# Sum jobs kept out of the stretch from attention's end to the end of the values' block, and the second half of that block's input forms queued behind attention's output product

## The chip, the core and the metric

The kernel runs on one core of one Trainium2 chip, in one launch. The metric is the device time of that launch in microseconds. Engines: PE (TensorE, matmuls), PEld (its weight loads), DVE (VectorE), ACT (ScalarE), POOL (GpSimd) and SP (SyncE, which here only issues transfers). Each engine works through its own list of instructions in order. A DMA is issued from the list of SP, ACT or POOL, and is carried out by the core's 16 DMA engines.

## The reference

Two layers of a decoder trunk on 512 tokens of width 1024, in float32, and a final normalization. The heart of a layer:

```python
h = rmsnorm(x, g_mix)
z = h @ w_in
aq, ak, av, rq, rk, rv, rg, ga, gb = jnp.split(z, SPLIT_POINTS, axis=-1)
ya = sliding_window_sink_attention(rope(aq), rope(ak), av, sinks) @ w_a
r = chunkwise_retention(rotate(rq), rotate(rk) * (RET_QK_DIM ** -0.5), rv)
yb = (group_rms(r) * jax.nn.silu(rg)) @ w_b
x = x + (jax.nn.sigmoid(ga) * ya + jax.nn.sigmoid(gb) * yb) @ w_out
x = x + jnp.square(jax.nn.relu(rmsnorm(x, g_mlp) @ w_up)) @ w_down
```

(Names shortened where the shape is plain.) `rv`, the retention's values, is a product of the 512 x 1024 input and a 1024 x 1024 part of `w_in`.

## The kernel before

**Three matmuls for one.** Each float32 product is made of three in a rounded format: a weight and an input are each split into a high and a low part, and `products` (L387 to L389) multiplies high by high, low by high and high by low. A weight comes as units of 128 x 1024 in the fixed order of `unit_order`. SP loads a unit into one of five `raw` tiles; ScalarE copies it into `hi` (L335) and VectorE subtracts into `lo` (L336), `SPLIT` = 3 units ahead of use; loads run `AHEAD` = 4 units ahead of the split.

**Seven products for eight.** The values, and the two large products of the MLP, are computed by blocks in a scheme of Strassen's kind: sums of weight blocks are multiplied by sums of input blocks. The sums of weights are made by DMA alone and lie in memory as `sums_rv`, `sums_up`, `sums_down` and `sums_last`. `sum_steps` is the list of these jobs for one layer, in the order of use: two for the values, then for each of the MLP's eight blocks two of `w_up` and one of `w_down`. A job is two DMAs from POOL's queue: a copy of the first half of the data (L223) and an accumulation of the second half onto it (L226). The accumulation can be issued only when the copy has landed. One step of the list issues the copy of a job and then the accumulation of the job before it.

**What paces them.** `pace` (L242) is called where a result leaves PSUM. On every second call, while the list lasts, it has POOL copy one column of that result into `mark` (L247), so that POOL waits for it, and puts the next step behind this mark on POOL. Before the change it is called, per layer, at the eight chunks of gate a, the eight of the retention's queries and keys, the eight of its gate, the eight of attention's output product (L1132), the eight of gate b, the eight of `mixed` and the eight of the new `x`: 56 calls, 28 steps. The list of layer 0 needs 26 steps, that of layer 1 needs 24.

**The stretch in question.** Attention is a generator of 16 iterations (four blocks of 128 queries, four pairs of heads) and some more that empty its pipeline; its parts are laid between the matmuls of the chunks by `advance`. The code then runs in this order (names as used below): the eight gate chunks; rk0 and rq0 (the retention's head 0); rg0 to rg3 (four chunks of its gate); the rest of attention (`drain`); `turned.load(0)`; rk1 and rq1; `turned.build(0)`; `turned.load(2)`; rg4 and rg5; `turned.build(2)`; attention's output product; the values (`values`); rk2, rq2, rk3, rq3; and so on.

`Turned` makes the sums of input blocks for the values. `load(ks)` fetches two 128 x 1024 tiles `xg` of the layer's input from memory, from POOL's queue (L871). `build(ks)` scales them on ScalarE (L881, four instructions), takes four sums on VectorE (L884 to L887), and makes three splits, each a copy on ScalarE (L407) and a subtraction on VectorE (L408). Both `build` calls stand in a `tc.issue_after` on attention's last split, so their instructions on ScalarE and VectorE come behind it in those engines' lists. `xg` takes two of six large temporary tiles, which the gate's chunks, the tables and attention's results use as well.

Attention's output product is four units of `w_a` with two chunks of 12 matmuls each; VectorE multiplies each chunk into `mixed` (L1131), which gives its PSUM bank back. PE has five such banks. In `values`, `multiply(a, ...)` reads plain input blocks, `multiply(c, turned[1])` is the first to read the sums, from both `build` calls; `add_values` adds two weight blocks (L315) for two of its seven parts.

**Order.** A planner lays out each engine's list from the program's order and dependencies and an estimate of durations; `tc.issue_after(ins)` makes what is inside it come behind `ins` on `ins`'s engine. So the order on an engine can differ from the text, and it is to be read from the trace.

**The last edit's place.** In layer 1, `turn_x` (L1236) writes the layer's `x`, turned, to memory as the start of the output `y`: eight tiles, each copied from PSUM by ScalarE into one of seven temporaries of 128 x 512 (L1248) and sent from POOL (L1249). `gain_tile` is a tile of four such parts, of which the final gain uses the first two.

Of the kernel before, what the change touches and what calls it, by code (L numbers as in the profile page):

```python
# [12 lines left out]
AF = mybir.ActivationFunctionType  # L13
ALU = mybir.AluOpType
# [8 lines left out]
NB = T // P  # L23
# [92 lines left out]
def decoder(ctx, tc, xT, x_first, w_in, w_rv, w_a, w_b, w_out, w_up, w_pair, w_down, w_end, tables, decay, band, g_last, out):  # L116
    nc = tc.nc
# [13 lines left out]
    def temp(name="t"):  # L131
        return tmp.tile([P, T], F32, tag="t", name=name, bufs=7)
# [31 lines left out]
    state = {"next": 0, "loaded": 0, "split": 0, "hold": None}  # L164
# [74 lines left out]
    DONE, steps = object(), []  # L239
    pace_count = [0]  # L240

    def pace(src):  # L242

        pace_count[0] += 1
        if steps and pace_count[0] % 2 == 0:
            mark = small.tile([P, 1], F32, tag="mark", name="mark", bufs=2)
            ins = nc.gpsimd.tensor_copy(mark, src[:, 0:1])  # L247
            with tc.issue_after(ins.ins):
                if next(steps[0], DONE) is DONE:
                    steps.pop(0)  # L250
# [66 lines left out]
    def split_until(n):  # L317
        while state["split"] < min(n, len(order)):
            i = state["split"]
            name, part = order[i][1], order[i][-1]  # L320
            if name == "rv":
                add_values(i)
            load_until(i + AHEAD)
            if name == "pair":
                add_part(i)
            elif name == "block":
                add_block(i)
            raw = raws[i]
            hi = wpool.tile([P, UNIT], F32R, tag="hi", name="hi", bufs=SPLIT + 1)
            lo = wpool.tile([P, UNIT], F32R, tag="lo", name="lo", bufs=SPLIT + 1)  # L330
            for at in (LEFT,) if name == "pair" and part == 3 else halves(i):
                if i == 0 and at.start == 0:
                    nc.vector.tensor_copy(hi[:, at], raw[:, at])
                else:
                    nc.scalar.activation(hi[:, at], raw[:, at], AF.Copy)  # L335
                nc.vector.tensor_tensor(lo[:, at], raw[:, at], f32(hi[:, at]), ALU.subtract)  # L336
            kept = {
                "pair": part < 2,
                "block": name == "block" and part < 4 and order[i][2] < N_BLOCK - 1,
                "rv": name == "rv" and order[i][2] < 4,  # L340
            }
            if not kept.get(name):
                raws.pop(i)
            parts[i] = (hi, lo)
            state["split"] += 1
# [265 lines left out]
    def layer_body(layer):  # L611
# [112 lines left out]
        def attention():  # L724
# [36 lines left out]
            for n in range(NB):  # L761
                w = P if n == 0 else 2 * P
                keys = slice(0, P) if n == 0 else slice((n - 1) * P, (n + 1) * P)
                at = slice(n * P, (n + 1) * P)
                for c in range(4):
                    col = layer * N_Q + 2 * c
                    ps = bank(ps_aux, "score")
# [5 lines left out]
                    sm = temp("sm")  # L773
# [22 lines left out]
                    for g in range(N_KV):  # L796
                        nc.vector.tensor_scalar(s3[:, g, :], s3[:, g, :], rc[:, g : g + 1], None, ALU.mult)
                    pend.append((n, c, sm))
                    if ready and c == 1 + DELAY:
                        weighted(ready.pop())  # L800
                    if len(pend) > DEEP:
# [13 lines left out]
        last_exp, last_split = [], []  # L815
# [11 lines left out]
        mixed = [x[:, c, :] for c in range(KD)]  # L827
# [26 lines left out]
        def qk(h, rate=1.0):  # L854
            chunk("w_in", layer, xs, put_ret(rk, h), rate)
            chunk("w_in", layer, xs, put_ret(rq, h), rate)
# [250 lines left out]
        source = xT if layer == 0 else spill  # L1107
        turned = Turned()
        turned.load(0)
        qk(1)  # L1110
        with tc.issue_after(last_split[0]), tc.issue_after(last_split[1]):
            turned.build(0)
        turned.load(2)
        for i in (4, 5):
            chunk("w_in", layer, xs, put_rg(i))
        with tc.issue_after(last_split[0]), tc.issue_after(last_split[1]):
            turned.build(2)


        aT = [(a_h[:, c, :], a_l[:, c, :]) for c in range(4)]  # L1120
        for u in range(4):
            hi, lo = unit("w_a", layer)
            for j in range(2):
                c = 2 * u + j
                ps = bank(ps_mm, "mm")
                pairs = []
                for k in range(4):
                    cols = slice(k * 256 + j * P, k * 256 + (j + 1) * P)
                    pairs.append(((hi[:, cols], lo[:, cols]), aT[k]))
                products(ps, pairs, True, True)  # L1130
                nc.vector.tensor_tensor(mixed[c], mixed[c], ps, ALU.mult)  # L1131
                pace(mixed[c])  # L1132
        for t in a_t:
            slots.give(*t[1])

        load_decay(0)
        values(turned)
        background.append(retention(0))
        qk(2, 2.0)
        qk(3, 2.0)  # L1140
# [95 lines left out]
        def turn_x(ps, b, i):  # L1236
            for k in range(4):
                nc.tensor.matmul(
                    ps[:, k * P : (k + 1) * P],
                    x[:, 4 * i + k, b * P : (b + 1) * P],  # L1240
                    ident,
                    start=k == 0,
                    stop=k == 3,
                    is_transpose=True,
                    skip_group_check=True,
                )
            t = temp("y")
            nc.scalar.activation(t, ps, AF.Copy)  # L1248
            nc.gpsimd.dma_start(y[:, b, i * T : (i + 1) * T], t)  # L1249

# [541 lines left out]
```

## Time and profile before

| what | us |
|---|---|
| runs before (3): median, lowest, highest | 1491.83, 1490.25, 1492.48 |
| the profiled execution: its time | 1491.67 |
| the profiled execution: its span, first to last instruction | 1489.9 |
| chain of waits: share of PE | 86% |

The span is what the profile shows; the execution's time has 1.8 us around it. Timeline rows read: start, duration, engine, line of the kernel, operation, output and inputs, count, and in brackets the time that the engine stood idle before and what ended it. Rows of the DMA list end with size and microseconds from issue to landing. The page's rows of digits are 40 slices of the span in tenths.

### The profile page before, as it was taken

The numbers are of one execution on the slowest core, as the hardware profiler recorded it, in microseconds if no ns is written. First come the engines' busy times: TensorE is split into PE (matmuls) and PEld (weight loads), VectorE is DVE, ScalarE is ACT, GpSimd is POOL, SyncE is SP. The second block draws the span as 40 slices with busy tenths as digits, with TensorE's granted clock in tenths as the row PEclk, the third lists the DMA queues.
The fourth block names the chain that finished last, engine by engine and source line by source line (L and its number), as shares of the span: only waits on it lengthen the run. The fifth ranks groups of instructions, "written<-read, shape, count | busy, mean of one in ns | idle before, by whom it ended". The sixth has DMA issues, their size and how long they took to land.

```text
span 1489.9 us, 21378 instructions
## 1 busy us (share of the span) xinstructions
PE 1461.6 (98%) x7751; PEld 1259.5 (85%) x7751; DVE 1121.9 (75%) x1697; ACT 942.6 (63%) x1549; POOL 215.5 (14%) x302
## 2 busy tenths in 40 slices
PE   9999999999999999999999998899999999999998
PEld 7888778888889999998888886788888889999997
DVE  6877776866677888888878686768766768888885
ACT  7657555543467777777755574455435677777775
POOL 0101210102101111112101012002020021111120
PEclk9999999999999999999999999999999999999999
DMA  7673993658946777766948559936595277776664
GB/s 258 195 208 109 272 285 111 186 154 251 280 98 195 193 189 193 197 175 197 291 150 239 159 129 243 284 107 178 160 268 185 92 206 193 189 198 183 176 189 146
DMA packets 95867, 287.32 MB, mean 193 GB/s; under 512 B 11152, under 2 KB 11280, under 8 KB 90896
## 3 DMA queue, kind: packets, MB, share of 16 engines
q0 software_dynamic: 33648, 113.26, 34.0%
q1 hardware_dynamic: 61392, 171.37, 33.8%
q8 instruction: 61, 1.00, 0.3%
q10 hardware_dynamic: 720, 1.31, 0.2%
q14 instruction: 46, 0.38, 0.1%
HBM read 246.05 MB, written 107.48 MB: 237 GB/s over the span
## 4 chain that ended last, share of the span: by engine, by line
PE 86%; DMA 7%; ACT 3%; DVE 2%; issue 1%; POOL 0%; SPq 0%; ACTq 0%; DVEq 0%; POOLq 0%
PE mm L387 23%; PE mm L389 23%; PE mm L388 23%; PE b L387 3%; PE b L388 3%; PE b L389 3%; DMA raw<-w_rv_in 2%; DMA xg<-spill 1%; PE mm L402 1%; DMA xg<-xT_in 1%; PE score L770 1%; DVE lo L336 1%; DMA sums_down<-w_down_in 1%; ACT hi L335 1%; PE r L388 1%
## 5 line engine op out<-in xcount | busy, mean ns | idle before, releaser
L335 ACT ACTIVATE hi<-raw 128x1024 fp32r<-128x1024 f32 (+1 forms) x375 | 381.7, 1020 | 302.3 <-PE mm L388 165.5
L336 DVE TENSOR_TENSOR lo<-raw,hi 128x1024 fp32r<-128x1024 f32 (+1 forms) x376 | 437.7, 1172 | 151.9 <-ACT hi L335 150.9
L387 PE MATMUL mm<-xh,hi 128*128 128x512 f32 (+1 forms) x976 | 345.6, 356 | 7.3 <-ACT hi L335 5.4
L388 PE MATMUL mm<-xl,hi 128*128 128x512 f32 (+1 forms) x976 | 345.0, 356 | 0.0
L389 PE MATMUL mm<-xh,lo 128*128 128x512 f32 (+1 forms) x976 | 343.1, 356 | 1.5 <-DVE lo L336 1.5
L387 PE MATMUL mm<-r,hi 128*128 128x256 f32 (+1 forms) x736 | 237.1, 326 | 8.7 <-DVE x L1131 8.2
L389 PE MATMUL mm<-r,lo 128*128 128x256 f32 (+1 forms) x736 | 239.4, 325 | 0.3 <-DVE lo L336 0.3
L388 PE MATMUL mm<-r,hi 128*128 128x256 f32 (+1 forms) x736 | 239.6, 326 | 0.0
L387 PEld LDWEIGHTS mm<-xh,hi 128*128 128x128 f32 x976 | 185.5, 190 | 33.0 <-ACT hi L335 5.7
L389 PEld LDWEIGHTS mm<-xh,lo 128*128 128x128 f32 x976 | 184.7, 190 | 26.8 <-DVE lo L336 2.7
L388 PEld LDWEIGHTS mm<-xl,hi 128*128 128x128 f32 x976 | 185.7, 190 | 24.8
L387 PEld LDWEIGHTS mm<-r,hi 128*128 128x128 f32 x736 | 140.1, 190 | 23.0 <-DVE x L1131 9.0
L388 PEld LDWEIGHTS mm<-r,hi 128*128 128x128 f32 x736 | 140.2, 190 | 13.2
L389 PEld LDWEIGHTS mm<-r,lo 128*128 128x128 f32 x736 | 140.2, 190 | 11.9 <-DVE lo L336 0.5
L1474 POOL DMA_DIRECT2D y<-eu x56 | 62.3, 1351 | 371.5 <-DVE eu L1459 371.5
L388 PE MATMUL mm<-lo,r 128*128 128x512 f32 (+1 forms) x276 | 104.3, 387 | 0.0
L389 PE MATMUL mm<-hi,r 128*128 128x512 f32 (+1 forms) x276 | 101.2, 387 | 0.0
L387 PE MATMUL mm<-hi,r 128*128 128x512 f32 (+1 forms) x276 | 98.7, 391 | 1.8 <-ACT eu L1469 1.3
L387 PE MATMUL b<-hi,r 128*128 128x512 f32 x180 | 70.4, 391 | 0.0
L388 PE MATMUL b<-lo,r 128*128 128x512 f32 x180 | 70.2, 390 | 0.0
L271 DVE TENSOR_TENSOR raw<-raw 128x512 f32<-128x512 f32 x56 | 38.5, 687 | 39.5 <-DMA raw<-w_pair_in 27.2
L389 PE MATMUL b<-hi,r 128*128 128x512 f32 x180 | 67.8, 389 | 0.0
(294 smaller groups left out, 2404.1 us busy)
## 6 DMA issues: line engine op xcount, KB each, us to landing
raw<-w_in_in SPq DMA_DIRECT2D x73, 512.0 KB, 4.8
sums_down<-w_down_in POOLq DMA_DIRECT2D x30, 1024.0 KB, 12.5
sums_up<-w_pair_in POOLq DMA_DIRECT2D x56, 512.0 KB, 10.7
raw<-w_down_in SPq DMA_DIRECT2D x45, 512.0 KB, 7.2
raw<-w_pair_in SPq DMA_DIRECT2D x84, 256.0 KB, 3.6
y<-y POOLq DMA_DIRECT2D x64, 256.0 KB, 9.0
y<-eu POOLq DMA_DIRECT2D x62, 256.0 KB, 8.1
raw<-sums_down SPq DMA_DIRECT2D x30, 512.0 KB, 7.1
```

The lines of the kernel that those rows point to most:

```text
L271: nc.vector.tensor_tensor(raws[i][:, at], last[:, LEFT], last[:, RIGHT], ALU.add)
L335: nc.scalar.activation(hi[:, at], raw[:, at], AF.Copy)
L336: nc.vector.tensor_tensor(lo[:, at], raw[:, at], f32(hi[:, at]), ALU.subtract)
L387: nc.tensor.matmul(ps, ah, bh, start=start and i == 0, stop=False, **more)
L388: nc.tensor.matmul(ps, ah, bl, start=False, stop=False, **more)
L389: latest[0] = nc.tensor.matmul(ps, al, bh, start=False, stop=stop and i == n - 1, **more).ins
L402: latest[0] = nc.tensor.matmul(ps, w[:, cols(j, c)], moving[k][low], start=first, stop=bool(final)).ins
L770: nc.tensor.matmul(ps[:, g * w : (g + 1) * w], q_s[g][:, c, at], part[:, keys], start=i == 0, stop=i == 1)
L1474: nc.gpsimd.dma_start(y[:, 2 * j + m, i * T : (i + 1) * T], t, **how)
```

## The change

```diff
+    quiet = [False]
+
     def pace(src):
 
+        if quiet[0]:
+            return
         pace_count[0] += 1
...
-                    nc.scalar.activation(hi[:, at], raw[:, at], AF.Copy)
+                    state["high"] = nc.scalar.activation(hi[:, at], raw[:, at], AF.Copy).ins
...
                     pend.append((n, c, sm))
+                    if n > 1:
+                        pace(sm)
...
         turned.load(0)
+        quiet[0] = True
         qk(1)
         with tc.issue_after(last_split[0]), tc.issue_after(last_split[1]):
             turned.build(0)
         turned.load(2)
         for i in (4, 5):
             chunk("w_in", layer, xs, put_rg(i))
-        with tc.issue_after(last_split[0]), tc.issue_after(last_split[1]):
-            turned.build(2)
...
-                nc.vector.tensor_tensor(mixed[c], mixed[c], ps, ALU.mult)
-                pace(mixed[c])
+                last_mixed = nc.vector.tensor_tensor(mixed[c], mixed[c], ps, ALU.mult)
+            if u == 1:
+                with tc.issue_after(last_mixed.ins), tc.issue_after(state["high"]):
+                    turned.build(2)
         for t in a_t:
             slots.give(*t[1])
 
         load_decay(0)
         values(turned)
+        quiet[0] = False
...
-            t = temp("y")
+            t = gain_tile[:, 2 + i, :] if b == NB - 1 else temp("y")
```

Four things change. From the first input load of `Turned` to the end of `values`, `pace` does nothing, so no step of the sum jobs is issued from the results in between. In attention's iterations of its third and fourth block (`n > 1`), `pace` is called with the score tile `sm`. The second `build` is traced inside the output product, after its second unit, and its instructions come behind that unit's last multiplication into `mixed` on VectorE and behind the newest whole-unit copy into `hi` on ScalarE. And the last two tiles of `turn_x` go through the free half of `gain_tile`.

## The prediction

> **What bounds the kernel now.** I read the page first, then the waits of the matrix engine, its timeline wherever it stood idle, the windows around those places, and last the timelines of the queues that feed them.
>
> ```profile
> span 1489.9 us, 21378 instructions
> ...
> PE 1461.6 (98%) x7751; PEld 1259.5 (85%) x7751; DVE 1121.9 (75%) x1697; ACT 942.6 (63%) x1549; POOL 215.5 (14%) x302
> ...
> DMA  7673993658946777766948559936595277776664
> ...
> PE 86%; DMA 7%; ACT 3%; DVE 2%; issue 1%; POOL 0%; SPq 0%; ACTq 0%; DVEq 0%; POOLq 0%
> ```
>
> PE is the bound: 1461.6 of 1489.9 us, so nothing that leaves the matmuls alone can win more than the 28.3 us of idle time, plus what the clock loses around it. A slice of the DMA row is 1489.9/40 = 37.2 us. Slices 4 and 5 (149 to 223 us) and 24 and 25 (894 to 969 us) stand at 9, with 3 (112 to 149 us) and 5 just ahead of them. Those pairs are the stretch that the change touches, once in each layer. PE's idle time lies just there:
>
> ```profile
> 170.44 0.50 PE L387 MATMUL mm<-r,hi 128*128 128x512 f32 x1 [2.49 <-DVE x L1131]
> 220.58 0.50 PE L387 MATMUL mm<-xh,hi 128*128 128x512 f32 x1 [2.24 <-ACT hi L335]
> 222.19 0.50 PE L389 MATMUL mm<-xh,lo 128*128 128x512 f32 x1 [0.88 <-DVE lo L336]
> 909.17 0.79 PE L387 MATMUL mm<-r,hi 128*128 128x512 f32 x1 [5.73 <-DVE x L1131]
> 961.20 0.79 PE L387 MATMUL mm<-xh,hi 128*128 128x512 f32 x1 [3.17 <-ACT hi L335]
> 963.07 0.80 PE L389 MATMUL mm<-xh,lo 128*128 128x512 f32 x1 [0.64 <-DVE lo L336]
> 1192.99 0.50 PE L387 MATMUL mm<-hi,r 128*128 128x512 f32 x1 [1.32 <-ACT eu L1469]
> ```
>
> Two kinds of stall, each in both layers. In attention's output product PE waits for VectorE's multiplication into `mixed` (L1131), which frees a bank: 2.49 + 5.73 = 8.22 us. Towards the end of the values' block it waits for the split of a weight: 2.24 + 0.88 + 3.17 + 0.64 = 6.93 us. The clock adds to them:
>
> ```profile
> 222.00:226.00 4.00, 3.81 (x11) 3.04 (x12) 4.00 (x8) 1.47 (x3) 0.00 (x0) 0.65 0.55 189
> 226.00:230.00 4.00, 4.00 (x18) 3.27 (x17) 0.99 (x3) 0.00 (x0) 0.00 (x0) 0.93 0.44 131
> ...
> 910.00:914.00 4.00, 4.00 (x13) 3.13 (x13) 3.53 (x5) 2.34 (x3) 0.56 (x1) 0.67 1.02 251
> ...
> 962.00:966.00 4.00, 3.36 (x8) 2.38 (x8) 4.00 (x7) 1.98 (x4) 0.00 (x0) 0.50 0.67 242
> 966.00:970.00 4.00, 4.00 (x16) 3.22 (x16) 1.87 (x4) 0.00 (x0) 0.00 (x0) 0.84 0.44 141
> ```
>
> (Columns: the stretch, its width, busy time of PE, PEld, DVE, ACT and POOL, granted clock, DMA share, GB/s.) After each of these stalls but the one at 170 the granted clock is low for some microseconds. Width times (1 - clock): 1.40 + 0.28 and 2.00 + 0.64, so 4.3 us behind the values' stalls, and 1.3 us behind the one at 909. The Trainium skill (TensorE: Matmul & The Clock Gate, Part 1: The HAM clock gate) says that the gate halves the clock after an idle window of about 3.4 us; the trace agrees for 5.73 us idle (0.67) and for 2.49 us (no drop), and by that rule a stall that only gets shorter would cost its own length and nothing more.
>
> What is behind the stalls is transfers:
>
> ```profile
> 144.58 14.05 DMA xg<-xT_in
> ...
> 203.40 13.97 DMA raw<-w_rv_in
> ...
> 945.01 10.79 DMA raw<-w_rv_in
> ```
>
> ```profile
> raw<-w_in_in SPq DMA_DIRECT2D x73, 512.0 KB, 4.8
> sums_down<-w_down_in POOLq DMA_DIRECT2D x30, 1024.0 KB, 12.5
> sums_up<-w_pair_in POOLq DMA_DIRECT2D x56, 512.0 KB, 10.7
> ```
>
> On the chain of waits a 512 KB load of the values' weights takes 13.97 and 10.79 us, where the same size takes 4.8 us in the median of `w_in`. Beside them run the sum jobs, on POOL's queue (rows of layer 0):
>
> ```profile
> 137.81 0.64 POOL L247 COPY mark<-late 128x1 f32<-128x1 f32 x1 [44.82 <-ACT late L407]
> 138.38 0.53 POOL L223 DMA_DIRECT2D sums_up<-w_pair_in  x1
> ...
> 139.87 1.09 POOL L223 DMA_DIRECT2D sums_down<-w_down_in  x1
> 144.03 0.85 POOL L226 DMA_DIRECT2D sums_up<-w_pair_in  x1 [3.08 <-DMA sums_up<-w_pair_in]
> 144.58 1.42 POOL L871 DMA_DIRECT2D xg<-xT_in  x2
> ...
> 152.83 0.86 POOL L226 DMA_DIRECT2D sums_down<-w_down_in  x1 [6.20 <-DMA sums_down<-w_down_in]
> 153.60 0.65 POOL L871 DMA_DIRECT2D xg<-xT_in  x1
> ...
> 171.28 0.57 POOL L871 DMA_DIRECT2D xg<-xT_in  x1 [4.63 <-DVE r L408]
> ...
> 202.65 0.81 POOL L226 DMA_DIRECT2D sums_down<-w_down_in  x1 [11.62 <-DMA sums_down<-w_down_in]
> ```
>
> POOL issues in order, so a second half of a job (L226) that waits for its first half holds all behind it. The last row is a 1 MB accumulation that starts 0.75 us ahead of the weight load at 203.40.
>
> **The change part by part.**
>
> *Silence (`quiet`).* Per layer 12 calls of `pace` fall silent: rk1, rq1, rg4, rg5 and the eight chunks of the output product. Every second call makes a step, so 6 steps go: 6 marks, 6 copies, 6 accumulations, between the second group of input loads and the end of the values. One accumulation stays open over the silence. This takes the sum traffic off the values' loads. Need, from the trace: layer 0's load at 203.40 must land early enough to lift 2.24 us, layer 1's at 945.01 3.17 us early; at 4.8 us instead of 13.97 and 10.79 they land 9.2 and 6.0 us early. So I take all of the values' stalls and their clock away: 6.93 + 4.3 = **11.2 us**. Bounds: 0, if the loads are slow for other reasons (SP's own loads alone), and 11.2. I take the upper one because a slice at 9 holds six steps of 1 to 2 MB beside SP's loads.
>
> *Earlier jobs.* Eight calls more per layer, in attention's blocks 2 and 3: 4 steps. POOL stood idle 44.82 us ahead of 137.81 and the DMA row is at 3 there, so the marks and copies cost nothing on PE as long as POOL is free; if it is not, a mark holds its score tile, one of seven temporaries. By the order of the calls four of a layer's steps (3 and 4 or 6, and 7 and 8) are marked by a score tile. A step that follows another closely waits for its copy, 10.7 to 12.5 us by the rows above; a tile behind it is held for what is left of that. I take 0, because a tile waits several iterations for its transpose anyway, and up to 3 us a layer if it binds. In all 26 steps are left of 28; layer 0's list needs 26, layer 1's 24, so all sums are still made, two steps later, long before the blocks that read the last ones.
>
> *`build(2)` queued later.* It is 4 scalings and 3 splits on ScalarE, 4 + 3 operations on VectorE, now behind the product's fourth multiplication on VectorE and behind the newest weight split on ScalarE; no instruction is added. Before, its scalings stood ahead of `build(0)`'s own splits:
>
> ```profile
> 908.59 1.33 ACT L881 ACTIVATE xg<-xg,x 128x512 f32<-128x512 f32 x2 [2.94 <-DMA xg<-spill]
> ```
>
> ```profile
> 902.48 0.69 DVE L884 TENSOR_TENSOR xg<-xg 128x512 f32<-128x512 f32 x1 [8.46 <-ACT xg L881]
> ...
> 908.44 0.68 DVE L1131 TENSOR_TENSOR x<-x,mm 128x512 f32<-128x512 f32 x1
> ...
> 925.93 1.82 DVE L408 TENSOR_TENSOR r<-xg,r 128x512 fp32r<-128x512 f32 x2
> ```
>
> The 2.94 us wait on ScalarE goes. But the first multiplication (908.44), which ends PE's 5.73 us, came out of VectorE's backlog after 8.46 us of waiting for `build(0)`'s input, not for `build(2)`'s. So the product's stalls hang on when the first input loads land. Bounds: 0 (same landing) and 8.22 + 1.3 = 9.5 us (landing 6 us earlier). Nothing in the trace settles POOL's new order, so I take the middle, **4.8 us**. The second input loads need a buffer that `build(0)` frees (171.28 waits for it); the wait moved from ScalarE's queue to behind the product has PE's work of half a product (48 matmuls) and the values' first multiplication (24) over it, which at the spacing of these two rows is 72 x 0.23 = 16.6 us:
>
> ```profile
> 929.99 0.39 PE L387 MATMUL rv<-hi,r 128*128 128x512 f32 x1
> 930.22 0.39 PE L388 MATMUL rv<-lo,r 128*128 128x512 f32 x1
> ```
>
> The first of them is the first matmul of the values' second multiplication, which reads the forms. If that cover is gone, PE waits there (C below).
>
> *`gain_tile` for the last two turned tiles (layer 1).* Two temporaries fewer in the ring. The 1.32 us at 1192.99 is the only stall there; bounds 0 and 1.3, I take **0.4**, as ScalarE had just come from those two copies in its own order and the edit does not move them.
>
> Sum: 11.2 + 4.8 + 0.4 = 16.4 us. Against the profiled execution's own 1491.67 us: 1475.3. That execution lies 0.16 us under the median of the runs (1491.83), so 1475.4 on their scale.
>
> **The rivals.**
>
> *A: POOL's queue holds the first input loads back (slower).* With four steps more before it, the step at rq0 (137.81) starts the third block of `w_down`, 1 MB, and the step at rg1 must accumulate it. Before, that place held a 512 KB job, whose accumulation waited until 144.03 and let the input loads out at 144.58. A 1 MB half takes 12.5 us in the median: 138.4 + 12.5 + 0.8 = 151.7, 7.1 us later, in both layers. If the input loads then take their 14.05 us again, the product's stalls become 9.6 and 12.8 us, with some 1.7 us of clock in layer 0 (as after the stalls at 222): + 15.9, less the 11.2 and 0.4 = + 4.3 us, 1496. It decides from a delay of (11.6 - 1.7) / 2 = 5 us a layer. For it: POOL's rows in that order. Against it: before, the accumulation of a 1 MB job (152.83) was queued behind the first input loads, so the planner that lays out POOL's order may do so again; and later loads would meet a quieter DMA. The Trainium skill (DMA: Bandwidth & Descriptors, Anatomy of one DMA) states that a wait on a semaphore happens on the issuing sequencer before dispatch, not in the DMA engines; the row at 152.83 agrees, and by that rule everything behind such an accumulation is late by its wait.
>
> *B: only the values' stalls go.* The first input loads land as late as before, later issue and quieter DMA cancelling: 11.2 + 0.4, or 8 with a remainder of the moved waits: 1480 to 1484.
>
> *C: the wait moves into the values.* In layer 1 `build(2)`'s first split stood at 925.93 on VectorE, 4.1 us before the second multiplication began (929.99). If PE arrives 7 us earlier and the forms come no earlier, PE waits about 3 us plus 1.3 of clock: of 16.4 us some 12 remain, 1480, inside B's range. Against it: `build(0)` no longer waits 2.94 us, so the buffer, the load and the forms come earlier too.
>
> *D: it does nothing that counts.* SP's own loads saturate the stretch: 1489 to 1493.
>
> **How the numbers follow.** Forecast 0.52 (values' stalls gone, the product's shortened: gains of 11.6 to 21, so 1470.5 to 1480); B and C together 0.25; A 0.15, spread from 1487 to 1499; D 0.08. What a measurement can tell from no change is about 0.2%, 3 us. Faster: 0.52 + 0.25, with a little of A: 0.78. Same: most of D and a part of A: 0.09. Slower: the rest of A: 0.13. The range from 1469 to 1492 leaves out the worse two thirds of A and the edges of the others, less than 2 in 10.
>
> **What would show it.** DMA rows: slices 4, 5, 24, 25 fall below 9, slice 3 rises, POOL shows no `sums_` rows from about 155 to 235 us. Values: no PE wait for L335 or L336 near 220 and 960, the weight load on the chain under 8 us, clock 1.00 there. Product: PE's waits for L1131 together under 8.22 us; A shows as an input load issued near 151 and 891 us behind a waiting `sums_down` accumulation, and L1131 waits above 9 us. C shows as PE waiting for L408 on `r<-xg` before `rv`. The prediction is wrong at its root if the values' loads still take over 10 us without sum jobs beside them, or if the total falls by less than 8 us.

## The result, and the profile after

| what | before | after |
|---|---|---|
| median of 7 runs each, us | 1491.83 (1489.31 to 1494.99) | 1485.09 (1482.37 to 1487.99) |
| ratio, 95% interval | | 0.9956 [0.9939, 0.9972] |
| the profiled execution: time, span, us | 1491.67, 1489.9 | 1483.84, 1482.1 |

The change makes the kernel 6.7 us faster, less than half of the 16.4 us of the forecast. The page after, with the rows that answer to those of before:

```profile
span 1482.1 us, 21386 instructions
...
DMA  7659643668975676666957595546598277777664
...
PE 89%; DMA 5%; ACT 3%; DVE 1%; issue 1%; POOL 0%; POOLq 0%; DVEq 0%; ACTq 0%
```

Slices 4, 5, 24 and 25 of the DMA row fell from 9 to 6, 4, 5 and 5; those just ahead, 3 and 23, stand at 9 instead. PE's stalls in the timeline after, in the same places:

```profile
146.36 0.47 PE L759 MATMUL pv<-r,r 128*128 128x512 f32 x1 [1.57 <-DVE r L412]
173.85 0.79 PE L391 MATMUL mm<-r,hi 128*128 128x512 f32 x1 [3.51 <-DVE x L1136]
909.27 0.80 PE L391 MATMUL mm<-r,hi 128*128 128x512 f32 x1 [5.86 <-DVE x L1136]
1198.39 0.39 PE L393 MATMUL mm<-r,lo 128*128 128x256 f32 x1 [0.44 <-DVE lo L340]
```

(The lines moved: L1136 is the multiplication into `mixed`, before L1131; L391 to L393 the three matmuls; L887 and L890 to L893 `build`; L877 its loads; L251 the mark.) The values' four stalls (6.93 us) are gone, and with them the slow loads of the values' weights. From the DMA lists, first before, then after:

```profile
raw<-w_rv_in SPq DMA_DIRECT2D x12, 512.0 KB, 9.8
```

```profile
raw<-w_rv_in SPq DMA_DIRECT2D x12, 512.0 KB, 4.1
```

The product's stalls are not gone: 9.37 us in all for 8.22. A new one of 1.57 us stands in attention. The stretches show the clock as well. First the kernel before, then the one after (columns as in the prediction):

```profile
140.00:180.00 40.00, 37.51 (x166) 30.73 (x165) 29.08 (x43) 21.54 (x32) 11.09 (x19) 1.00 0.97 277
180.00:240.00 60.00, 56.88 (x251) 46.81 (x249) 44.94 (x56) 32.00 (x42) 5.43 (x10) 0.97 0.82 234
...
900.00:980.00 80.00, 70.46 (x294) 57.18 (x293) 58.84 (x76) 42.28 (x58) 13.74 (x19) 0.91 0.84 236
```

```profile
140.00:180.00 40.00, 34.92 (x141) 27.75 (x140) 26.26 (x38) 20.13 (x30) 6.10 (x11) 0.91 0.85 234
180.00:240.00 60.00, 60.00 (x270) 49.82 (x269) 47.68 (x59) 33.32 (x44) 0.00 (x0) 1.00 0.40 129
...
900.00:980.00 80.00, 74.14 (x330) 61.45 (x329) 63.25 (x84) 47.07 (x66) 0.54 (x1) 0.96 0.46 143
```

Take width less PE's busy time for the idle part, and width times (1 - clock) for the slow part. 140 to 180: 2.5 us lost before, 5.1 + 3.6 = 8.7 after. 180 to 240: 3.1 + 1.8 = 4.9 before, nothing after. 900 to 980: 9.5 + 7.2 = 16.7 before, 5.9 + 3.2 = 9.1 after. Together 24.1 before and 17.8 after: 6.3 of the 7.8 us between the two spans. (Where the clock is low while PE stands idle, as at 0.73 from 904 to 908 before, the time counts in both parts; this makes each total some 2 us too high and hardly touches the difference.) So one stretch wins, one loses, and the third wins in part. Why 140 to 180 lost is on the chain of waits after:

```profile
138.11 12.04 DMA sums_down<-w_down_in
...
150.74 0.50 POOL sums_down L226
151.27 11.60 DMA xg<-xT_in
162.90 1.34 ACT xg L887 x2
...
173.19 0.61 DVE x L1136
```

The first input loads are issued at 151.27, after a 1 MB accumulation has waited for its copy; before, at 144.58. They take 11.60 us, and 10.3 us pass from their first scaling on ScalarE to the multiplication that PE waits for. VectorE between these two:

```profile
165.67 0.69 DVE L890 TENSOR_TENSOR xg<-xg 128x512 f32<-128x512 f32 x1 [7.69 <-ACT xg L887]
166.62 1.23 DVE L340 TENSOR_TENSOR lo<-raw,hi 128x1024 fp32r<-128x1024 f32 x1 [0.26 <-ACT hi L339]
...
169.57 0.68 DVE L892 TENSOR_TENSOR xg<-xg 128x512 f32<-128x512 f32 x1
170.17 0.69 DVE L893 SCALAR_TENSOR_TENSOR xg<-t,xg 128x512 f32<-128x512 f32 x1
...
173.11 0.68 DVE L1136 TENSOR_TENSOR x<-x,mm 128x512 f32<-128x512 f32 x1
```

The multiplication needs nothing of `build(0)`, but VectorE's list has nearly all of `build(0)` ahead of it, and two weight splits: it comes 7.44 us after the start of `build(0)`, which had waited 7.69 us. So three things could carry the stall: the late issue, the slow landing, and this order. The new wait in attention is a different one:

```profile
144.42 0.47 POOL L251 COPY mark<-z 128x1 f32<-128x1 f32 x1
...
144.92 0.69 DVE L995 TENSOR_TENSOR z<-z,sig 128x512 f32<-128x512 f32 x1 [4.71 <-POOL mark L251]
```

`silu` overwrites a gate chunk in place (L995), and the mark reads that chunk. POOL, still waiting for an accumulation (143.89), reads it late; VectorE waits 4.71 us, and behind it stand the splits that attention's matmul at 146.36 needs.

### The profile page after: what moved, and what is told of

The parts are those of the page before. It is cut to its first block, busy times and chain, and to the rows that moved or that the text cites. A ratio compares the mean times of both kernels' runs of the same rounds, so it can differ in the third digit from the quotient of the medians.

```text
span 1482.1 us, 21386 instructions
## 1 busy us (share of the span) xinstructions
PE 1459.7 (98%) x7751; PEld 1259.0 (85%) x7751; DVE 1124.0 (76%) x1697; ACT 943.1 (64%) x1549; POOL 213.0 (14%) x302
## 4 chain that ended last, share of the span: by engine, by line
PE 89%; DMA 5%; ACT 3%; DVE 1%; issue 1%; POOL 0%; POOLq 0%; DVEq 0%; ACTq 0%
PE mm L391 23%; PE mm L393 23%; PE mm L392 23%; PE b L391 3%; PE b L392 3%; PE b L393 3%; PE rv L393 2%; PE rv L392 2%; PE rv L391 2%; PE mm L406 1%; DMA xg<-spill 1%; DMA sums_up<-w_pair_in 1%; PE score L774 1%; DMA sums_down<-w_down_in 1%; DMA xg<-xT_in 1%
## 5 line engine op out<-in xcount | busy, mean ns | idle before, releaser
L391 PE MATMUL mm<-xh,hi 128*128 128x512 f32 (+1 forms) x976 | 344.0, 355 | 1.6 <-DVE z L985 1.0
L393 PE MATMUL mm<-xh,lo 128*128 128x512 f32 (+1 forms) x976 | 341.6, 355 | 0.0
L391 PE MATMUL mm<-r,hi 128*128 128x256 f32 (+1 forms) x736 | 238.6, 328 | 9.8 <-DVE x L1136 9.4
L393 PE MATMUL mm<-r,lo 128*128 128x256 f32 (+1 forms) x736 | 240.7, 327 | 0.4 <-DVE lo L340 0.4
L391 PEld LDWEIGHTS mm<-xh,hi 128*128 128x128 f32 x976 | 184.8, 189 | 26.7 <-ACT xh L414 1.4
L393 PEld LDWEIGHTS mm<-xh,lo 128*128 128x128 f32 x976 | 183.8, 189 | 23.8
L391 PEld LDWEIGHTS mm<-r,hi 128*128 128x128 f32 x736 | 141.1, 192 | 24.3 <-DVE x L1136 10.1
L393 PEld LDWEIGHTS mm<-r,lo 128*128 128x128 f32 x736 | 140.9, 191 | 12.3 <-DVE lo L340 0.6
L393 PE MATMUL mm<-hi,r 128*128 128x512 f32 (+1 forms) x276 | 101.2, 387 | 0.0
L391 PE MATMUL mm<-hi,r 128*128 128x512 f32 (+1 forms) x276 | 98.7, 391 | 0.5 <-ACT r L411 0.2
L391 PE MATMUL b<-hi,r 128*128 128x512 f32 x180 | 70.5, 392 | 0.0
L393 PE MATMUL b<-hi,r 128*128 128x512 f32 x180 | 67.8, 389 | 0.0
```

The lines of the kernel that those rows point to most:

```text
L391: nc.tensor.matmul(ps, ah, bh, start=start and i == 0, stop=False, **more)
L393: latest[0] = nc.tensor.matmul(ps, al, bh, start=False, stop=stop and i == n - 1, **more).ins
```

## The experiments

Ratios are against the kernel before, run on the same chip in the same batch (medians 1492.66, 1493.14, 1491.63 and 1491.99 us for the four batches: e1, e2, e3 and e6; e4, e7, e8 and e9; e5, e10 and e11; e12).

### Parts of the change

**e3: silence and the earlier jobs alone.** The kernel before with `quiet` and the calls in attention; `build(2)` at its old place, no `gain_tile`.

```diff
 # kernel before
+        if quiet[0]:
+            return
...
+                    if n > 1:
+                        pace(sm)
...
         turned.load(0)
+        quiet[0] = True
...
         values(turned)
+        quiet[0] = False
```

> The kernel before with the silence and the calls in attention alone; the second build stays where it was, and so do the last two turned tiles. Theory: the values' weights land in under 6 us and the values' waits (6.93 us) and their slow clock are gone; the product's waits are those of the changed kernel or up to 2 us longer, because the second build's scalings stand ahead on ScalarE: 1485 to 1488. Rival (the moved build is what pays): 1489 to 1492 with values' waits left.

Measured: 1485.41 us, 0.9947 [0.9931, 0.9964]. That is the whole gain of the change (0.9956): what e3 leaves out, the moved `build(2)` and `gain_tile`, adds nothing to it that can be measured. No stall is left in the values; PE's waits for the product are 7.1 us (1.93 and 5.14), and the new wait in attention is there (1.65).

**e4: the moved `build(2)` alone.** In the kernel before, the call goes behind the product's second unit.

```diff
 # kernel before
-        with tc.issue_after(last_split[0]), tc.issue_after(last_split[1]):
-            turned.build(2)
...
+            if u == 1:
+                with tc.issue_after(last_mixed.ins), tc.issue_after(state["high"]):
+                    turned.build(2)
```

> The kernel before with only the second build moved into the output product and queued behind its fourth multiplication; jobs as before. If the 2.94 us that ScalarE waited for the second loads had held PE: the waits for the multiplication into mixed fall by 2 to 4 us from 8.2, 1488 to 1490. If the landing of the first loads sets them: 7.5 to 8.5 us, the values' waits (6.9 us) unchanged or up to 2 us longer, 1491 to 1494.

Measured: 1490.77 us, 0.9986 [0.9976, 0.9995], some 2 us. The product's waits are 7.6 us (2.09 and 5.46) for 8.22, a difference that e5 will show to be within what two executions differ by. What the move frees on ScalarE is hardly on PE's path, as VectorE's list still has `build(0)` ahead of the multiplications.

**e5: `gain_tile` alone.**

```diff
 # kernel before
-            t = temp("y")
+            t = gain_tile[:, 2 + i, :] if b == NB - 1 else temp("y")
```

> The kernel before with only the gain_tile edit. By the prediction's term 0.4 us less (0 to 1.3): 1491.0 to 1492.5 beside a before of about 1492.5. If the 1.32 us wait for eu at 1193 goes, the edit carries it; if it stays, the wait vanished in the changed kernel through the earlier arrival of something else.

Measured: 1490.73 us, 0.9991 [0.9982, 1.0001]. The 1.32 us wait for `eu` is gone, and one of 0.51 us for a split stands at 1203.55 instead. By the waits it is worth 0.8 us, by the times 0.9, no more than a run can tell from nothing. As this edit touches nothing before 1190 us, e5 also shows how far two executions differ there, with the same order on the engines: PE's waits for the product are 6.5 us in it (1.55 and 4.94), 8.22 in the kernel before. So a difference of one or two microseconds in these waits shows nothing by itself.

**e2: silence without the earlier jobs.** The changed kernel without the calls in attention; the steps that are lost are caught up by calling `pace` twice at each chunk of `x`, at the end of the layer's first half.

```diff
 # changed kernel
-                    if n > 1:
-                        pace(sm)
...
                 pace(x[:, c, :])
+                pace(x[:, c, :])
```

> The changed kernel without the calls in attention; the list is finished by a second call at each chunk of the new x instead (26 steps as before). The place ahead of the first input loads then holds a 512 KB job again. Theory: the loads are issued near 144.6 and 884 us as in the kernel before, no wait of VectorE for a mark, no wait of PE for attention's last transposes (1.57 us), L1136 waits at or under the 8.2 us of before, in layer 0 under 3; the time is 2 to 6 us under the changed kernel (1479 to 1483). Rival (full DMA engines): the same as the changed kernel within 1.5 us, L1136 at 9 us. Both expect no wait for the values' weights.

Measured: 1488.19 us, 0.9961 [0.9944, 0.9978]. The wait for the mark and the one in attention are gone, the input loads issue at 145.67 and 891.5 us, the product's waits fall to 6.75 us (2.26 and 4.49). But the jobs now run into the MLP of layer 0, where PE waits for splits, 5.9 us in all; the longest of these in the timeline:

```profile
464.31 0.58 PE L393 MATMUL mm<-r,lo 128*128 128x256 f32 x1 [3.90 <-DVE lo L340]
```

The ratio is that of the change (0.9956), as the rival had it, but not for its reason: the product's waits did fall, and the MLP took the gain. Placed there, behind attention, the jobs cost as much as ahead of it. (The profiled execution, 1490.75 us, is the slowest of eight; the fastest took 1483.35, and its waits are not known.)

### Issue, traffic or order

**e1: the first input loads from SP's queue**, so that no accumulation on POOL stands ahead of them.

```diff
 # changed kernel
             def load(self, ks):
+                queue = nc.gpsimd if ks else nc.sync
...
-                    nc.gpsimd.dma_start(b, source[:, k : k + 2, :])
+                    queue.dma_start(b, source[:, k : k + 2, :])
```

> The changed kernel with the first two input loads (ks = 0) issued from SP's queue instead of POOL's, so that they no longer stand behind the accumulation of the 1 MB job. Theory (POOL's queue: the loads are late because their issue is late, 151.27 and 888.53 us): they are issued at 141 to 146 us, land 3 to 8 us earlier, the product's waits for L1136 fall from 9.4 us together to under 4, and the time falls by 4 to 9 us against the changed kernel (1476 to 1481). Rival (the DMA engines are full there, the place of the issue does not matter): the loads land at 160 to 163 us as before, L1136 stays at 8 to 10 us, 1484 to 1486. Second rival (VectorE's order, not the landing, sets the first multiplication): landing earlier, L1136 waits unchanged.

Measured: 1484.29 us, 0.9946 [0.9924, 0.9967]; the waits are 9.4 us again (5.39 and 3.98). A miss for the theory that POOL's queue is the price. SP issues them at 147.91 and 884.81, 3.4 and 3.7 us earlier, and they take longer, beside the same sum jobs; the DMA list:

```profile
xg<-xT_in SPq DMA_DIRECT2D x2, 512.0 KB, 15.6
...
xg<-spill SPq DMA_DIRECT2D x2, 512.0 KB, 15.3
```

**e6: silence from before rq0.** The changed kernel with `quiet` set ahead of rk0 and rq0 rather than behind rg3, the calls in attention from its second block on, and `pace` twice at each chunk of `x`, so that all sums are made.

```diff
 # changed kernel
+        quiet[0] = True
         qk(0, PACE)
...
         turned.load(0)
-        quiet[0] = True
...
-                    if n > 1:
+                    if n > 0:
...
                 pace(x[:, c, :])
+                pace(x[:, c, :])
```

> The changed kernel with the silence begun ahead of rk0 instead of after the first input loads, the calls in attention from its second block on, and a second call at each chunk of the new x (27 steps). No sum job stands on POOL within 30 us of the input loads. Theory: POOL issues the first loads as soon as a large buffer is free, near 141 to 145 us, they land in 5 to 9 us, the product's waits fall under 2 us together, the time is 7 to 11 us under the changed kernel (1474 to 1478). Rival (full DMA engines from SP's own loads): landing 11 us and more, L1136 at 6 us or more, under 3 us gained. Second rival (VectorE's order): landing early and L1136 waits unchanged.

Measured: 1474.70 us, 0.9881 [0.9860, 0.9902]: 18 us faster than before, about what was forecast for the change. No wait for the product, none in attention's end (four new waits, 4.4 us in all, stand earlier in layer 1's attention, from 803 to 856 us); the DMA share from 137 to 160 is 0.33 (1.02 in the changed kernel). POOL issues the first input loads at 114.51 and 143.01, and they land in 4.6 us; POOL's timeline and the DMA list:

```profile
114.51 0.77 POOL L877 DMA_DIRECT2D xg<-xT_in  x1
143.01 0.55 POOL L877 DMA_DIRECT2D xg<-xT_in  x1 [27.73 <-issue]
```

```profile
xg<-xT_in POOLq DMA_DIRECT2D x4, 512.0 KB, 4.6
xg<-spill POOLq DMA_DIRECT2D x4, 512.0 KB, 4.5
```

The order on VectorE is a new one too: 8.1 us pass from the first scaling to the first multiplication (156.8 to 164.9), 10.2 in the changed kernel. So e6 alone doesn't part the quiet from the order; e7, e10 and e11 do that.

**e9: e6 with `build(2)` at its old place** (the move of e4 undone in e6).

```diff
 # e6
             chunk("w_in", layer, xs, put_rg(i))
+        with tc.issue_after(last_split[0]), tc.issue_after(last_split[1]):
+            turned.build(2)
...
-            if u == 1:
-                with tc.issue_after(last_mixed.ins), tc.issue_after(state["high"]):
-                    turned.build(2)
```

> The kernel with the silence begun ahead of rk0, with the second build back at its old place ahead of the output product. It prices the move where the transfers are out of the way. If the move frees the first multiplication into mixed: PE waits for it 2 to 5 us over both layers, 1477 to 1481. If with quick loads the place does not matter: 1473 to 1476.5.

Measured: 1475.24 us, 0.9880 [0.9864, 0.9896]. With quick loads the move is worth nothing that can be measured.

**e7: e6 with the traffic put back, without the waiting.** Three pairs of plain copies of weights into unused memory, at the results that set off sum steps in the changed kernel; no accumulation, so POOL waits for none.

```diff
 # e6
+    def traffic(layer, n, src):
+        ins = nc.gpsimd.tensor_copy(mark, src[:, 0:1])
...
+        with tc.issue_after(ins.ins):
+            for half in range(2):
+                nc.gpsimd.dma_start(extra[layer][2 * n + half, :, :width], source[:, half * width // 2 : half * width // 2 + width])
```

(`width` is 2048 for the first pair, at rq0, and 1024 for those at rg1 and rg3.)

> The kernel with the silence begun ahead of rk0 (1474.70 us, no wait of PE for L1136), to which at rq0, rg1 and rg3 plain copies into scratch are added: two of 1 MB and four of 512 KB a layer, about what the changed kernel's three steps move there, with no accumulation and so no wait for a landing on POOL. Theory (traffic: the first input loads are slow because the sum jobs run beside them): the loads are issued by 146 us, take 10 to 15 us, and PE waits for the first multiplication into mixed 5 to 9 us over both layers; 1481 to 1486. Rival (queue: they are late because POOL waits for a landing ahead of them): the loads land by 152 us, PE waits under 2 us, 1474 to 1477.

Measured: 1476.58 us, 0.9890 [0.9867, 0.9912], and no wait for the product. The time is that of the rival and can't be told from e6's (0.9881), though the traffic does slow the loads, as the theory says; the DMA list, and VectorE's timeline from `build(0)` to the first multiplication (here L903 and L1151), with that of the kernel before below it:

```profile
xg<-xT_in POOLq DMA_DIRECT2D x4, 512.0 KB, 11.8
xg<-spill POOLq DMA_DIRECT2D x4, 512.0 KB, 11.4
```

```profile
162.72 0.69 DVE L903 TENSOR_TENSOR xg<-xg 128x512 f32<-128x512 f32 x1 [0.69 <-ACT xg L900]
...
166.87 0.68 DVE L1151 TENSOR_TENSOR x<-x,mm 128x512 f32<-128x512 f32 x1
167.47 0.69 DVE L905 TENSOR_TENSOR xg<-xg 128x512 f32<-128x512 f32 x1
```

```profile
162.61 0.69 DVE L884 TENSOR_TENSOR xg<-xg 128x512 f32<-128x512 f32 x1
...
166.76 0.68 DVE L886 TENSOR_TENSOR xg<-xg 128x512 f32<-128x512 f32 x1
...
169.71 0.68 DVE L1131 TENSOR_TENSOR x<-x,mm 128x512 f32<-128x512 f32 x1
```

`build(0)` starts within 0.11 us of where it starts in the kernel before (162.61), but the multiplication stands ahead of L905 (the third of `build(0)`'s sums, L886 before), and comes 4.15 us after the start where it took 7.10 us (162.61 to 169.71). Before, that gap ended in a stall of 2.49 us. So traffic beside loads that are issued at 142.1 makes no stall by itself, and the order on VectorE, which the planner lays out anew for each kernel, decides as much as the landing.

**e8 and e10: e6 with POOL held, without traffic.** A copy of 2 KB and 4 (e8) or 8 (e10) accumulations of 2 KB from rg1 on, the first input loads behind them on POOL.

```diff
 # e6
+    def hold(layer, src):
+        ins = nc.gpsimd.tensor_copy(mark, src[:, 0:1])
+        with tc.issue_after(ins.ins):
+            nc.gpsimd.dma_start(tiny, w_down[layer, 0][0:1, :512])
+            for _ in range(4):
+                held[:] = [nc.gpsimd.dma_start(tiny, w_down[layer, 0][0:1, :512], accum_op=ALU.add).ins]
...
-        turned.load(0)
+        with tc.issue_after(held[0]):
+            turned.load(0)
```

> The kernel with the silence begun ahead of rk0, in which POOL is held instead: at rg1 a copy of 2 KB and four accumulations of 2 KB, each waiting for the one before it to land, and the first input loads put behind the last. About 10 us of POOL's time and next to no traffic; the loads leave POOL near 150 us, as in the changed kernel (151.27). Theory (traffic): they then land in 4 to 6 us, by 156 us, before the 158.65 of the kernel before; PE waits for mixed under 3 us over both layers; 1475 to 1478. Rival (queue): PE waits 7 us and more, 1480 to 1485.

> Like e8, with 8 tiny accumulations instead of 4 ahead of the first input loads on POOL's queue: at some 2.4 us each the hold lasts to about 152 us in layer 0 and 890 us in layer 1, the issue times of the changed kernel (151.27, 888.53), with no sum traffic beside them. Theory 'late issue alone is the price' (rival A as it was worked out): PE waits for the product's multiplications again, 7 to 9.4 us in all, and the time is 1482 to 1487. Theory 'traffic sets the price, an issue at 151 is soon enough for a transfer of 4.5 us': the loads land near 156.5 and 895 us, as early as ScalarE scales them in e6 (156.8), the waits stay under 1 us, time 1474 to 1477.

Measured: e8 1474.72 us, 0.9877 [0.9863, 0.9892]; e10 1480.85 us, 0.9927 [0.9914, 0.9941]. Neither held for the time that was meant: in e8 the loads go out at 143.18, sooner than in the changed kernel, and nothing waits, so it tells only that quiet loads land in 4.4 us. In e10 they go out later than in the changed kernel, at 158.69 and 895.96, and PE waits:

```profile
171.89 0.50 PE L402 MATMUL mm<-r,hi 128*128 128x512 f32 x1 [1.19 <-DVE x L1150]
...
909.90 0.50 PE L402 MATMUL mm<-r,hi 128*128 128x512 f32 x1 [2.44 <-DVE x L1150]
```

Issued 7.4 us later than in the changed kernel, they land at the same time (first scaling at 163.1, there 162.9), so what the quiet saves on the way the late issue takes back. In layer 0 the wait is 1.19 us where it is 3.51: VectorE comes to the multiplication 8.1 us after that scaling and not 10.2, with the third sum behind it. In layer 1 the two can't be compared, as PE itself comes to the product 4 us later in e10 (907.46 for 903.41), after a wait of 1.43 us for another instruction of VectorE (L647). The time is 6 us above e6's and between the two forecasts: an issue this late costs even when all is quiet. The lateness of the changed kernel, 151.27, would not by itself: at 4.4 us of transfer the loads would land at 155.7, ahead of the 156.8 at which e6 scales without any stall (an estimate, not run).

**e11: the multiplications first.** The changed kernel with `build(0)` queued behind the second multiplication of the product and `build(2)` behind the sixth; `load(2)` moves with `build(0)`, the first loads, the jobs and their traffic stay as they are.

```diff
 # changed kernel
-        with tc.issue_after(last_split[0]), tc.issue_after(last_split[1]):
-            turned.build(0)
-        turned.load(2)
...
-            if u == 1:
+            if u == 0:
+                with tc.issue_after(last_mixed.ins), tc.issue_after(state["high"]):
+                    turned.build(0)
+                turned.load(2)
+            if u == 2:
                 with tc.issue_after(last_mixed.ins), tc.issue_after(state["high"]):
                     turned.build(2)
```

> The changed kernel with build(0) queued behind the second multiplication of the output product and build(2) behind the sixth; loads, sum jobs and their traffic as in the changed kernel. Theory 'the product waits only because its multiplications stand behind build(0) in VectorE's queue, and build(0) waits for the input': PE's waits for the product's multiplications fall from 9.4 us to under 1.5, their slow clock (about 4.4 us) goes, the loads still take 11 to 14 us; time 1473 to 1477. Rival 'the forms are needed that early': PE waits instead for the forms at the head of the values' block, 4 us or more a layer, and the time stays 1481 to 1486.

Measured: **1473.02 us**, 0.9874 [0.9860, 0.9887]: 18.6 us under before, the lowest median of all, with an interval that overlaps those of e6 to e9. PE's list of waits has no multiplication of the product any more, and only 1.3 + 0.2 us in the values, which head the list:

```profile
PE rv L392 <- DVE lo L340: 1.3, 2, 0.8
```

The loads are no better for it (issued at 149.94, first scaling at 164.0, later than in the changed kernel), but the first multiplication no longer stands behind them:

```profile
162.79 0.69 DVE L1133 TENSOR_TENSOR x<-x,mm 128x512 f32<-128x512 f32 x1 [0.42 <-PE mm L393]
...
168.33 0.68 DVE L1133 TENSOR_TENSOR x<-x,mm 128x512 f32<-128x512 f32 x1
168.92 0.69 DVE L890 TENSOR_TENSOR xg<-xg 128x512 f32<-128x512 f32 x1
```

**e12: the same order without silence.** The edit of e11 on the kernel before, whose sum jobs go on through the stretch.

```diff
 # kernel before
-            turned.build(0)
...
-            turned.build(2)
...
+            if u == 0:
+                with tc.issue_after(last_mixed.ins), tc.issue_after(state["high"]):
+                    turned.build(0)
+                turned.load(2)
+            if u == 2:
+                with tc.issue_after(last_mixed.ins), tc.issue_after(state["high"]):
+                    turned.build(2)
```

> The kernel before, its sum jobs unsilenced, with build(0) queued behind the second multiplication of the output product and build(2) behind the sixth (as in e11). If VectorE's order carries the product's stalls by itself, PE's waits for the product's multiplications (8.2 us) and their slow clock (1.3 us) go while the values' stalls (6.9 us and 4.3 us of clock) stay: 1481 to 1484 beside a before of about 1492. If the values' block then waits for the forms or for loads still later beside the sum jobs, the values' waits grow by 3 us or more and the time is 1485 to 1493.

Measured: 1499.81 us, 1.0051 [1.0037, 1.0065], 8 us slower and above both forecasts. The product's stalls are gone, and the values pay for them; POOL, ScalarE and PE in layer 0, then PE in layer 1:

```profile
179.08 0.85 POOL L226 DMA_DIRECT2D sums_down<-w_down_in  x1 [4.30 <-DMA sums_down<-w_down_in]
179.66 0.82 POOL L871 DMA_DIRECT2D xg<-xT_in  x1
```

```profile
191.60 1.33 ACT L881 ACTIVATE xg<-xg,x 128x512 f32<-128x512 f32 x2 [13.40 <-DMA xg<-xT_in]
```

```profile
200.14 0.79 PE L387 MATMUL rv<-hi,r 128*128 128x512 f32 x1 [7.75 <-ACT rv L954]
...
946.89 0.80 PE L387 MATMUL rv<-hi,r 128*128 128x512 f32 x1 [14.42 <-ACT rv L954]
```

The second input loads, which in e11 find POOL idle (174.65 and 176.47, scaled from 178.77 on), wait behind accumulations here and land beside the jobs. ScalarE stands 13.40 us before their scaling, with the copies between two of the values' banks (L954), which the next product adds onto, behind it. So the order is worth its gain only where the silence keeps POOL and the DMA engines free.

### One table

First of the first input loads issued, first scaling on ScalarE, first multiplication of the product on VectorE, and PE's wait for it, us in layer 0 / layer 1:

| kernel | issue | scaling | multiplication | PE waits |
|---|---|---|---|---|
| before | 144.6 / 884.1 | 158.7 / 897.4 | 169.7 / 908.4 | 2.49 / 5.73 |
| after | 151.3 / 888.5 | 162.9 / 902.1 | 173.1 / 908.5 | 3.51 / 5.86 |
| e1, from SP | 147.9 / 884.8 | 162.5 / 898.6 | 173.9 / 907.2 | 5.39 / 3.98 |
| e7, traffic | 142.1 / 882.2 | 158.8 / 897.1 | 166.9 / 904.6 | none |
| e10, held | 158.7 / 896.0 | 163.1 / 901.1 | 171.2 / 909.2 | 1.19 / 2.44 |
| e6, quiet (second of them: 143.0 / 877.6) | 114.5 / 861.7 | 156.8 / 890.3 | 164.9 / 898.4 | none |
| e11, product first | 149.9 / 881.4 | 164.0 / 894.7 | 162.8 / 892.8 | none |

The wait depends also on when PE comes to the product, which differs between the kernels, in layer 1 above all. From scaling to multiplication layer 0 takes 10.2 to 11.5 us in the first three rows, and 8.1 in e7, e10 and e6.

## Why the prediction was right or wrong

**The values' stalls (11.2 us): right.** All four waits and the slow clock behind them are gone; the values' weight loads land in a median of 4.1 us after, and the forecast had set 4.8. e3 shows that the silence brings it without the other edits, save the earlier jobs. Rival D, that SP's own loads fill the stretch, is out with it: they alone keep the DMA engines at a share of 0.40 from 180 to 240 us.

**The first input loads (`build(2)` and "the middle, 4.8 us"): the step that failed.** The prediction saw that the product's stalls hang on the first input loads, and that VectorE's backlog stood on them, yet it bounded that term by 0 and 9.5 us, both gains, with "later issue and quieter DMA" left to the rivals. What the runs showed in its place: the loads go out and land later than before, not earlier (first scaling 4.2 and 4.7 us later), and the term brings nothing. In the profiled execution it is a loss: waits 9.37 for 8.22, so 1.15 us, and the clock. Behind the stall at 173.85 the clock is 0.50 and 0.80 in two stretches of 4 us, 2.8 us, where before it lost nothing; behind 909.27 it is 0.57 for 0.67, 0.4 us:

```profile
174.00:178.00 4.00, 4.00 (x10) 3.13 (x11) 4.00 (x6) 0.81 (x2) 0.11 (x1) 0.50 0.65 203
178.00:182.00 4.00, 4.00 (x16) 3.17 (x15) 2.83 (x5) 2.81 (x4) 0.00 (x0) 0.80 0.00 0
...
910.00:914.00 4.00, 4.00 (x12) 3.14 (x11) 4.00 (x7) 3.66 (x5) 0.54 (x1) 0.57 0.15 40
```

That is 4.3 us lost where 4.8 were to be gained, 9.1 us; by the profiled executions the forecast was out by 8.6 us in all, by the medians 9.7. That nothing was gained is shown by e3 as well; the size of the loss is that of two executions, and e5 shows that these waits alone can differ by 1.7 us with nothing changed in the stretch. The quieter DMA begins only behind these loads: they still run at a share of 1.02 from 137 to 160 us. e6 shows what comes of it when silence begins ahead of them, e11 when the multiplications do not stand behind them; either lifts the product's stalls whole. The move of `build(2)` itself is worth some 2 us alone (e4) and nothing beside quick loads (e9).

**Rival A: its mechanism came, its price did not.** The 1 MB job at rq0, the accumulation at rg1 and the loads behind it came as worked out, at 151.27 us (151.7 by the prediction), behind an accumulation that had waited 5.39 us. This agrees with the rule of the Trainium skill (DMA: Bandwidth & Descriptors, Anatomy of one DMA) that was set beside it, that the wait is on the issuing sequencer. But A let each microsecond of delay through to PE and put the waits at 22.4 us; they are 9.37. In layer 1 the issue is 4.5 us later, the first scaling 4.7, the first multiplication 0.1 (908.5 for 908.4), since there the list of VectorE has the multiplication ahead of L892, while before L886, L887 and a split stood ahead of it:

```profile
908.54 0.68 DVE L1136 TENSOR_TENSOR x<-x,mm 128x512 f32<-128x512 f32 x1
909.13 0.68 DVE L892 TENSOR_TENSOR xg<-xg 128x512 f32<-128x512 f32 x1
```

A also took POOL's place for the cause; e1 shows that the place alone is not, and e7 that the traffic alone is not. The stall comes where the multiplication stands behind `build(0)` on VectorE and `build(0)`'s input comes late: e11 takes the first away, e6 the second for the most part, and either lifts it. How much of the 9.37 us is late issue and how much slow transfer stays open.

**Rival B came nearest.** It kept the product's stalls as before and set 1480 to 1484. It missed by 1 us, as its late issue and quieter DMA do not cancel: the loads land later, still beside the jobs.

**Earlier jobs at no cost: wrong by 1.6 us.** The prediction looked for a score tile held by its mark. What was held is a gate chunk that is overwritten in place; its cover, "POOL is free", failed at 143.89, and VectorE's 4.71 us became 1.57 on PE. e2 without these jobs has neither; e11 with them has 0.73.

**`gain_tile` (0.4): inside its bounds of 0 to 1.3**, 0.8 by the waits of e5, which a run can't tell from nothing.

**C, the wait moving into the values**, does not occur in the changed kernel. e12 shows it at full size, 7.75 and 14.42 us, and with it that the silence is what kept it away.

Sum as measured: 11.2 - 4.3 - 1.6 + 0.9 (the wait at 1192.99 less that at 1198.39) = 6.2 of the 7.8 us between the two profiled spans. The rest, 1.6 us, is not assigned. The median fell by 6.7 us, under the 8 us that the prediction had set as a sign of being wrong at its root; the other such sign, values' loads that stay over 10 us, did not come.

## What to carry to other kernels

When traffic is taken out of a stretch, see which loads the stretch depends on and begin the silence ahead of those: here the silence, begun ahead of rk0 and rq0 instead of behind rg3, with its jobs spread to either side, was worth 18 us and not 7. Read the list of the engine that frees a bank: an instruction that needs nothing of a late load still waits if the planner has put that load's users ahead of it. And test edits together: the order of e11 gains 12 us on the silenced kernel and loses 8 on the other.

## What the runs showed that was not expected

A 512 KB load beside the sum jobs takes 11 to 16 us whichever queue issues it (POOL 11.60, SP 15.6), and 4.6 without them. A one-column read on POOL can stop VectorE for 4.71 us when the tile it reads is overwritten in place.

Stalls of like length differ in what the clock does. 2.49 us (before, at 170.44) and 1.93 us (e3, at 173.52) leave it at 1.00, and so does the 1.57 us at 146.36; in e3 the same place waits 1.65 us, and the clock falls:

```profile
146.00:150.00 4.00, 3.42 (x10) 2.45 (x11) 4.00 (x7) 0.59 (x1) 0.00 (x0) 0.73 1.06 223
150.00:154.00 4.00, 4.00 (x17) 3.21 (x16) 3.19 (x5) 3.40 (x6) 2.78 (x5) 0.84 0.96 261
```

The Trainium skill (TensorE: Matmul & The Clock Gate, Part 1: The HAM clock gate) puts the drop behind an idle window of about 3.4 us and calls the window free-running; by the first alone 1.65 us should be free, and the measurement says that it is not always. The prediction's own rows had said so: behind waits of 2.24 and 0.88 us the clock stood at 0.65.
